# Side transfers issued in pieces between weight loads, and a norm's cross-channel sum four steps later, in a one-core hybrid decoder layer

## The chip, the core and the metric

One NeuronCore of a Trainium2 chip runs the whole layer. The metric is the device time of one execution in microseconds. Besides the repeated runs there is one execution taken with the hardware profiler; all rows of a view come from that one. In it the engines are TensorE (PE for the matmuls, PEld for its weight loads), VectorE (DVE), ScalarE (ACT), GpSimd (POOL) and SyncE (SP); a name with a q (SPq, ACTq) is an engine's sequencer, for example when it issues a DMA.

## The reference

For one sequence of 256 tokens of width 2048, in float32:

```
xn    = rms_norm(x, norm_mix_g)
proj  = xn @ w_in                     # u_s5, u_lru, q, k, v and three gates
gates = sigmoid(gate_logits + b_gate)
y_s5  = S5 branch: 64 groups, diagonal complex scan over time, gelu, GLU
y_lru = RG-LRU branch: causal conv, gated linear scan
y_att = stick-breaking attention, 8 heads of 128
merged = g_s5*(y_s5 @ w_br_s5) + g_lru*(y_lru @ w_br_lru) + g_attn*(y_att @ w_br_attn)
h  = x + merged @ w_out
h  = h + relu(rms_norm(h, norm_mlp_g) @ w_up)**2 @ w_down
out = rms_norm(h, final_norm_g)
```

## The kernel before

**The weight stream.** All weights are cut into 520 units of 256 x 512 values (512 KB), in one list that is also the order of use. A unit goes through four places. `load_next` (L130) issues its DMA on SP into one of three `raw` buffers. `split_next` makes two halves of it: ACT casts it to fp32r as `hi` (L146), DVE subtracts to get the rest, `lo` (L147); `hi` and `lo` have three buffers each. Then PE multiplies hi x hi, lo x hi and hi x lo: 12 matmuls of 512 columns for one unit (`chunk_tok`, L241 to L243; `pair_tok`, L276 to L278), or 24 of 256 (`chunk`, L225 to L227). A `raw` buffer is free once `lo` is made, and SP waits for that before the next load; `hi` and `lo` are free once PE is through with the unit. Units are numbered from 0 here: "unit 40" is the first of `w_br_lru`, "unit 232" the first of `w_out`, "unit 264" the first of `w_up`.

**Side work.** Everything else is written as generators. `later(gens, rate)` puts one on a list, and `pump()`, which is called after each unit, advances every listed generator by `rate` steps (a step ends at a `yield`). Each step is anchored behind the instructions of the unit just recorded. From this recorded program the framework's scheduler makes one fixed list for each engine at build time; SP's list is therefore one first-in, first-out queue in which weight loads and side transfers stand between each other, and an entry that waits holds all behind it.

**The places that the change touches.**

- `s5_scan`: for the first of eight blocks `s5_split(0)` makes `ux`, and `s5_stack(t)` for t = 0 to 3 copies parts of it into `stk` with three DMAs each (L627). PE's `ps_v` matmuls (L651) read `stk`, ACT copies their result to `s_v` (L653). For the later blocks the stacking is already spread over the steps of the scan.
- `gates`: for each of 12 chunks one row of `b_gate`, repeated over 128 partitions, is loaded to `gb` (L739, one buffer); DVE reads it when the chunk's matmuls are done (L744), and ACT takes the sigmoid (L745).
- the residual: `x_tok` (`xres` in the views), 2 MB, is loaded by one DMA on ACT's queue (L918) when the S5 pools are closed; DVE adds it to the result of `w_out` (L957). `gfb`, the last norm's gain repeated over 128 partitions (1 MB), is loaded by another one on ACT's queue (L989) and is first read near the end.
- `norm2`: the squares of the residual are summed by DVE over the channel tiles (L947, and two halvings at L972 in `hT`); then PE sums over partitions against a column of ones (`ps_n`, L977), and `rsqrt_mean` makes the scale `rs2`, which is not read before the first result of `w_down`.

Of the kernel before, what the change touches and what calls it, by code (L numbers as in the profile page):

```python
# [14 lines left out]
P = 128  # L15
# [3 lines left out]
CH = 512  # L19
# [27 lines left out]
def hybrid_block(ctx: ExitStack, tc: tile.TileContext, io, out):  # L47
    nc = tc.nc
# [115 lines left out]
    def later(gens, rate):  # L164
        side.append([deque(gens), rate, 0.0])
        return side[-1]
# [215 lines left out]
    def v2(t):  # L382
        return t.rearrange("p (a l) -> p a l", a=2)
# [10 lines left out]
    def repeat(a, n):  # L394
        r, w = a.shape
        return bass.AP(a.tensor, a.offset, [[w, r], [0, n], [1, w]])
# [219 lines left out]
    def s5_split(ct):  # L616
        bx = [ux[:, 2 + i, :].rearrange("p (r g s) -> p r g s", r=2, g=2) for i in range(2)]
        nc.scalar.copy(ux[:, 0, :], us5[:, ct, :])
        nc.vector.tensor_tensor(ux[:, 1, :], us5[:, ct, :], ux[:, 0, :].bitcast(F32), ALU.subtract)
        for g in range(2):  # L620
            m = mask[:, g:g + 1]
            nc.scalar.activation(bx[0][:, :, g, :], bco[:, ct], AF.Copy, scale=m)
            nc.vector.scalar_tensor_tensor(bx[1][:, :, g, :], bco[:, ct], m, bx[0][:, :, g, :].bitcast(F32), ALU.mult, ALU.subtract)
# [7 lines left out]
    def s5_scan():  # L631
        v = ypool.tile([P, 2, NT, L], F32, tag="yhi", name="s5_v")
        t12 = ypool.tile([P, 2, NT, L], F32, tag="ylo", name="s5_t")
        vr, vi, t1, t2 = v[:, 0], v[:, 1], t12[:, 0], t12[:, 1]
        tabs, more = s5_tables(0)
        yield from more
        s5_split(0)
        yield
        yield
        for t in range(NT):  # L640
            s5_stack(t)
        for _ in range(4):
            yield
        tt = nc.vector.tensor_tensor
        for b in range(WT):
            c, s = tabs
            t3 = pp.tile([P, NT, L], F32, tag="t3", name=f"t3_{b}")
            for t in range(NT):
                ps = pss.tile([P, CH], F32, tag="ps", name=f"ps_v{b}")
                for i in range(2):  # L650
                    nc.tensor.matmul(ps[:, i * L:(i + 1) * L], stk[:, t, 1, i * P:(i + 1) * P], stk[:, t, 0, :], start=i == 0, stop=True,  # L651
                                     skip_group_check=True)
                nc.scalar.copy(v[:, :, t, :], v2(ps))  # L653
                if t % 2:
                    yield
            more = iter(())
            if b + 1 < WT:
                s5_split(b + 1)
                tabs, more = s5_tables(b + 1)
                yield  # L660
            tt(t1, vr, c, ALU.mult)
            yield
            tt(t2, vi, s, ALU.mult)
            yield
            tt(t1, t1, t2, ALU.add)
            yield
            tt(t3, vi, c, ALU.mult)
            yield
            tt(vr, vr, s, ALU.mult)
            yield  # L670
            tt(t3, t3, vr, ALU.subtract)
            next(more, None)
            yield
            for x_ in (t1, t3):
                for t in range(NT):
                    j = b * NT + t
                    tt_scan(x_[:, t, :], rad[:, j:j + 1].broadcast_to([P, L]), x_[:, t, :])
                    if b + 1 < WT and x_ is t1:
                        s5_stack(t)
                    yield  # L680
            next(more, None)
            tt(t2, t1, c, ALU.mult)
            yield
            tt(vr, t3, s, ALU.mult)
            next(more, None)
            yield
            tt(t2, t2, vr, ALU.subtract)
            yield
            tt(vi, t3, c, ALU.mult)
            yield  # L690
            tt(t1, t1, s, ALU.mult)
            yield
            tt(t1, t1, vi, ALU.add)
            yield
            yield
            ps = pss.tile([P, CH], F32, tag="ps", name=f"ps_y{b}")
            for k, w_ in enumerate((t2, t1)):
                for t in range(NT):
                    nc.tensor.matmul(ps[t * 32:t * 32 + 32, 0:L], ce[:, k, b * NT + t, :, :], w_[:, t, :], start=k == 0, stop=k == 1,
                                     skip_group_check=True, tile_position=(0, t * 32))  # L700
            nc.vector.scalar_tensor_tensor(us5[:, b, :], us5[:, b, :], dsk[:, b:b + 1], ps[:, 0:L], ALU.mult, ALU.add)
            if b % 2:
                gq.append(later([gelu(b)], 1.0))
# [32 lines left out]
    def gates(idx, c, alloc):  # L736
        gb = tmp.tile([P, CH], F32, tag="gbias", name=f"gb{idx}_{c}", bufs=1)
        o = idx * D + c * CH
        nc.sync.dma_start(gb, repeat(io["b_gate_row"][:, o:o + CH], P))  # L739
        banks = chunk_tok("w_in", GATE0 + 4 * idx + c, D, xs)  # L740
        gts = []
        for j in range(2):
            g = alloc(c, j).rearrange("p a l -> p (a l)")
            nc.vector.scalar_tensor_tensor(g, banks[j], rstd_tok[:, j:j + 1], gb, ALU.mult, ALU.add)  # L744
            nc.scalar.activation(g, g, AF.Sigmoid)  # L745
            gts.append(g)
        return gts
# [118 lines left out]
    for q in range(4):  # L866
        s = slice(2 * q, 2 * q + 2)
# [4 lines left out]
    for c in range(2):  # L872
        banks = chunk("w_glu", c, W, lambda kt: (yg_hi[:, kt, :], yg_lo[:, kt, :]))
        for j in range(2):
# [4 lines left out]
            s = slice(c * 4 + 2 * j, c * 4 + 2 * j + 2)  # L879
# [22 lines left out]
    for a in S5_TAIL:  # L902
        c = int(a[1])
# [11 lines left out]
    mlp = ctx.enter_context(tc.tile_pool(name="mlp", bufs=1))  # L915
    gp = small("norm_mlp_g")
    x_tok = mlp.tile([P, 2, D], F32, name="xres")
    nc.scalar.dma_start(x_tok, io["x_res"])  # L918
    mf.append(chained(mq, split_tok(3, mlp.tile([P, 4, L], F32, tag="reluT", name="mT3", bufs=2))))
    hT = act.tile([P, KT, L], F32, tag="m16", name="hT")  # L920
    hhi = act.tile([P, KT, L], F32R, tag="xhi", name="hhi")
# [46 lines left out]
    def norm2():  # L968
        while rq[0]:
            yield  # L970
        for n in (2, 1):
            nc.vector.tensor_tensor(hT[:, 0:n, :], hT[:, 0:n, :], hT[:, n:2 * n, :], ALU.add)  # L972
        yield
        a = hT[:, 0, :]
        ps = pss.tile([P, CH], F32, tag="ps", name="ps_n2")
        for t in range(2):
            nc.tensor.matmul(ps[:, t:t + 1], a[:, t * P:(t + 1) * P], ones[:, 0:1], start=t == 0, stop=t == 1, skip_group_check=True)  # L977
        rsqrt_mean(rs2, ps[:, 0:2], 2)
        nc.vector.tensor_tensor(rs2, rs2, rs2, ALU.mult)
        yield  # L980

    tasks = [later([norm2()], 1.0)]


    gfb = mlp.tile([P, D], F32, name="gfb")
    ho = mlp.tile([P, 2, D], F32, name="ho")
    ssq = mlp.tile([P, 2, 6], F32, name="ssq")
    rf = mlp.tile([P, 2], F32, name="rf")
    nc.scalar.dma_start(gfb, repeat(io["final_norm_g"], P))  # L989

    def down_evac(t, s, bank):
        nc.vector.scalar_tensor_tensor(h_tok[:, t, s], bank, rs2[:, t:t + 1], h_tok[:, t, s], ALU.mult, ALU.add)
# [50 lines left out]
    for q in range(NQ):  # L1043
        hd, hf = {}, {}

        def up_done(cu, banks):
            c = cu % (FQ // CH)
            if c % 2 == 0:
                hd[c // 2] = (ypool.tile([P, WT, L], F32R, tag="yhi", name=f"hd_hi{q}_{c}"),
                              ypool.tile([P, WT, L], F32R, tag="ylo", name=f"hd_lo{q}_{c}"))  # L1050
            h_, l_ = hd[c // 2]
            r = mlp.tile([P, 2, CH], F32, tag="relu", name=f"relu{q}_{c}", bufs=2)
            for t in range(2):
                nc.scalar.activation(r[:, t, :], banks[t], AF.Relu)
            k = slice((c % 2) * 4, (c % 2) * 4 + 4)
            hf[c] = chained(hq, hidden(r, h_[:, k, :], l_[:, k, :], f"{q}_{c}"))

        if q == 0:
            pair_tok("w_up", 0, D, hs, up_done)
        for c in range(0 if q else 2, FQ // CH):  # L1060
            up_done(c, chunk_tok("w_up", q * (FQ // CH) + c, D, hs))

        def hs_(kt):
            need(hq, hf[kt // 4])
            h_, l_ = hd[kt // 8]
            return h_[:, kt % 8, :], l_[:, kt % 8, :]

        for task in tasks:
            finish(task)

        def down_done(c, banks):
            s = slice(c * CH, (c + 1) * CH)
            for t in range(2):
                down_evac(t, s, banks[t])
            if q == NQ - 1:
                for t in range(2):
                    square(t, s, c)
                    if c > 0:
                        total(t, c)
                    nc.gpsimd.tensor_tensor(ho[:, t, s], h_tok[:, t, s], gfb[:, s], ALU.mult)  # L1080

        pair_tok("w_down", 0, FQ, hs_, down_done)
        for c in range(2, 4):
            if q == NQ - 1 and c == 3:
                chunk_tok("w_down", c, FQ, hs_, HOLD, finish_tokens)
            else:
                down_done(c, chunk_tok("w_down", c, FQ, hs_))
# [67 lines left out]
```

## Time and profile before

| what | value |
|---|---|
| runs shown | 1517.03, 1522.82, 1524.22 us; median 1522.82 |
| profiled execution | 1518.29 us, of which the span from the first to the last instruction is 1516.4 us |
| PE / PEld busy | 1489.1 us (98%) / 1260.0 us (83%) |
| DVE / ACT / POOL busy | 1176.4 us (78%) / 783.9 us (52%) / 35.1 us (2%) |
| mean granted TensorE clock | 0.995 |
| DMA | 292.41 MB, mean 193 GB/s |

The profiled execution's own time is 1.9 us longer than its span, and 4.5 us under the median of the runs. A busy PE is not a PE at its peak: its matmuls overlap, so that one is recorded with about 390 ns while the next one starts 227 ns after it. A wait of PE is seen in the step from one matmul's start to the next one's.

### The profile page before, as it was taken

The numbers are of one execution on the slowest core, as the hardware profiler recorded it, in microseconds if no ns is written. First come the engines' busy times: TensorE is split into PE (matmuls) and PEld (weight loads), VectorE is DVE, ScalarE is ACT, GpSimd is POOL, SyncE is SP. The second block draws the span as 40 slices with busy tenths as digits, with TensorE's granted clock in tenths as the row PEclk, the third lists the DMA queues.
The fourth block names the chain that finished last, engine by engine and source line by source line (L and its number), as shares of the span: only waits on it lengthen the run. The fifth ranks groups of instructions, "written<-read, shape, count | busy, mean of one in ns | idle before, by whom it ended". The sixth has DMA issues, their size and how long they took to land.

```text
span 1516.4 us, 19895 instructions
## 1 busy us (share of the span) xinstructions
PE 1489.1 (98%) x7518; PEld 1260.0 (83%) x7518; DVE 1176.4 (78%) x1468; ACT 783.9 (52%) x920; POOL 35.1 (2%) x60
## 2 busy tenths in 40 slices
PE   9998999999999999999999999999999999999997
PEld 9996888989887878988787888888888888888886
DVE  6767988897988989689699797568855787558965
ACT  6767556565765564544355444344433444344443
POOL 1400000000000000000000000000000000000011
PEclk9999999999999999999999999999999999999999
DMA  9445766655555756565756556666666666666664
GB/s 291 152 151 180 214 205 201 187 182 170 176 174 179 211 185 210 185 204 187 268 179 189 185 181 207 194 191 198 193 195 192 192 190 198 191 194 192 193 196 152
DMA packets 88914, 292.41 MB, mean 193 GB/s; under 512 B 12786, under 2 KB 17010, under 8 KB 88562
## 3 DMA queue, kind: packets, MB, share of 16 engines
q1 hardware_dynamic: 88386, 287.93, 61.0%
q10 hardware_dynamic: 432, 3.21, 0.6%
q8 instruction: 59, 0.97, 0.3%
q14 instruction: 37, 0.30, 0.1%
HBM read 282.71 MB, written 2.10 MB: 188 GB/s over the span
## 4 chain that ended last, share of the span: by engine, by line
PE 81%; DVE 11%; issue 4%; ACT 2%; DMA 2%; SPq 0%; DVEq 0%; ACTq 0%
PE mt_w_up L242 6%; PE mt_w_up L243 6%; PE mt_w_up L241 6%; PE mt_w_in L242 5%; PE mt_w_in L243 5%; PE mt_w_in L241 5%; DVE lo L147 4%; PE mt_w_down L242 4%; PE mt_w_down L241 4%; PE mt_w_down L243 4%; PE mp_w_down L277 4%; PE mp_w_down L278 4%; PE mp_w_down L276 4%; PE mm_w_in L227 4%; PE mm_w_in L225 4%
## 5 line engine op out<-in xcount | busy, mean ns | idle before, releaser
L146 ACT CAST hi<-raw 128x1024 fp32r<-128x1024 f32 (+1 forms) x521 | 546.4, 1051 | 629.6 <-PE mt_w_up L243 131.6
L147 DVE TENSOR_TENSOR lo<-raw,hi 128x1024 fp32r<-128x1024 f32 (+1 forms) x521 | 638.2, 1226 | 289.4 <-ACT hi L146 285.6
L242 PE MATMUL mt_w_in<-lo,xhi 128*128 128x512 f32 x448 | 176.0, 393 | 3.5 <-DVE lo L147 3.4
L241 PE MATMUL mt_w_in<-hi,xhi 128*128 128x512 f32 x448 | 175.0, 395 | 0.2 <-ACT hi L146 0.2
L243 PE MATMUL mt_w_in<-hi,xlo 128*128 128x512 f32 x448 | 175.1, 391 | 0.0
L241 PE MATMUL mt_w_up<-hi,hhi 128*128 128x512 f32 x448 | 174.3, 389 | 0.0
L242 PE MATMUL mt_w_up<-lo,hhi 128*128 128x512 f32 x448 | 174.3, 389 | 0.0
L243 PE MATMUL mt_w_up<-hi,hlo 128*128 128x512 f32 x448 | 174.3, 389 | 0.0
L227 PE MATMUL mm_w_in<-xhi,lo 128*128 128x256 f32 x512 | 145.4, 286 | 4.7 <-DVE lo L147 4.7
L225 PE MATMUL mm_w_in<-xhi,hi 128*128 128x256 f32 x512 | 146.5, 286 | 0.4 <-ACT hi L146 0.4
L226 PE MATMUL mm_w_in<-xlo,hi 128*128 128x256 f32 x512 | 145.7, 285 | 0.0
L729 DVE STREAM_TRANSPOSE reluT<-relu 32x256 f32<-32x256 f32 x256 | 111.5, 435 | 4.2
L242 PEld LDWEIGHTS mt_w_in<-lo,xhi 128*128 128x128 f32 x448 | 84.6, 189 | 23.2 <-DVE lo L147 6.7
L227 PEld LDWEIGHTS mm_w_in<-xhi,lo 128*128 128x128 f32 x512 | 98.7, 194 | 5.7 <-DVE lo L147 5.7
L242 PE MATMUL mt_w_down<-lo,hd_hi 128*128 128x512 f32 (+1 forms) x272 | 102.5, 377 | 0.0
L241 PE MATMUL mt_w_down<-hi,hd_hi 128*128 128x512 f32 (+1 forms) x272 | 102.4, 377 | 0.0
L243 PE MATMUL mt_w_down<-hi,hd_lo 128*128 128x512 f32 (+1 forms) x272 | 102.4, 376 | 0.0
L277 PE MATMUL mp_w_down<-lo,hd_hi 128*128 128x512 f32 x256 | 99.8, 390 | 0.1
L225 PEld LDWEIGHTS mm_w_in<-xhi,hi 128*128 128x128 f32 x512 | 99.1, 194 | 0.9 <-ACT hi L146 0.7
L276 PE MATMUL mp_w_down<-hi,hd_hi 128*128 128x512 f32 x256 | 99.6, 389 | 0.0
L278 PE MATMUL mp_w_down<-hi,hd_lo 128*128 128x512 f32 x256 | 99.6, 389 | 0.0
L226 PEld LDWEIGHTS mm_w_in<-xlo,hi 128*128 128x128 f32 x512 | 99.2, 194 | 0.1
(299 smaller groups left out, 2356.1 us busy)
## 6 DMA issues: line engine op xcount, KB each, us to landing
raw<-in_w_in SPq DMA_DIRECT2D x175, 512.0 KB, 4.2
raw<-in_w_up SPq DMA_DIRECT2D x128, 512.0 KB, 4.3
raw<-in_w_down SPq DMA_DIRECT2D x128, 512.0 KB, 4.2
raw<-in_w_out SPq DMA_DIRECT2D x32, 512.0 KB, 4.2
raw<-in_w_br_lru SPq DMA_DIRECT2D x16, 512.0 KB, 4.2
raw<-in_w_br_attn SPq DMA_DIRECT2D x16, 512.0 KB, 3.9
raw<-in_w_br_s SPq DMA_DIRECT2D x16, 512.0 KB, 4.2
stk<-ux SPq DMA_DIRECT2D x96, 64.0 KB, 4.0
```

The costliest lines, as they stand in the source:

```text
L146: anchor["act"] = nc.scalar.copy(h[:, k, :], r[:, k, :]).ins
L147: anchor["dve"] = nc.vector.tensor_tensor(l_[:, k, :], r[:, k, :], h[:, k, :].bitcast(F32), ALU.subtract).ins
L225: nc.tensor.matmul(o, wh[:, kk, s], xh, start=first and ct % 2 == 0, stop=False, skip_group_check=True)
L226: nc.tensor.matmul(o, wh[:, kk, s], xl, start=False, stop=False, skip_group_check=True)
L227: mm = nc.tensor.matmul(o, wl[:, kk, s], xh, start=False, stop=last and ct % 2 == 1, skip_group_check=True)
L241: nc.tensor.matmul(banks[j], xh[:, s], wh[:, a:b], start=kt == 0, stop=False)
L242: nc.tensor.matmul(banks[j], xh[:, s], wl[:, a:b], start=False, stop=False)
L243: return nc.tensor.matmul(banks[j], xl[:, s], wh[:, a:b], start=False, stop=kt == ng * UK - 1)
L276: nc.tensor.matmul(o, xh[:, s], wh[:, kk, :], start=kt == 0, stop=False)
L277: nc.tensor.matmul(o, xh[:, s], wl[:, kk, :], start=False, stop=False)
L278: mm = nc.tensor.matmul(o, xl[:, s], wh[:, kk, :], start=False, stop=kt == ng * UK - 1)
L729: nc.vector.transpose(d_[32 * a:32 * a + 32, :, :, 32 * b:32 * b + 32], s_[32 * b:32 * b + 32, :, :, 32 * a:32 * a + 32])
```

## The change

Five edits, and nothing that is computed changes. The first block's stacking is issued with one step between the four groups of three DMAs. The gate's bias row is loaded by a side step three units after the chunk's start and no longer ahead of it. `x_tok` is loaded in four pieces of 512 KB on SP's queue, four steps apart, and no longer by one DMA on ACT's. `gfb` is loaded from SP and written at the second quarter of the MLP. And `norm2` has four steps, no longer one, between the sum over channel tiles and PE's sum over partitions.

```diff
@@ s5_scan
         for t in range(NT):
             s5_stack(t)
-        for _ in range(4):
             yield
@@ gates
         gb = tmp.tile([P, CH], F32, tag="gbias", name=f"gb{idx}_{c}", bufs=1)
         o = idx * D + c * CH
-        nc.sync.dma_start(gb, repeat(io["b_gate_row"][:, o:o + CH], P))
+
+        def bias():
+            for _ in range(3):
+                yield
+            nc.sync.dma_start(gb, repeat(io["b_gate_row"][:, o:o + CH], P))
+            yield
+
+        later([bias()], 1.0)
         banks = chunk_tok("w_in", GATE0 + 4 * idx + c, D, xs)
@@ residual
     x_tok = mlp.tile([P, 2, D], F32, name="xres")
-    nc.scalar.dma_start(x_tok, io["x_res"])
+
+    def x_load():
+        for c in range(4):
+            s = slice(c * CH, (c + 1) * CH)
+            nc.sync.dma_start(x_tok[:, :, s], io["x_res"][:, :, s])
+            for _ in range(4):
+                yield
+
+    later([x_load()], 1.0)
@@ norm2
             nc.vector.tensor_tensor(hT[:, 0:n, :], hT[:, 0:n, :], hT[:, n:2 * n, :], ALU.add)
-        yield
+        for _ in range(4):
+            yield
         a = hT[:, 0, :]
@@ the last norm's gain
-    nc.scalar.dma_start(gfb, repeat(io["final_norm_g"], P))
...
+        if q == 1:
+            nc.sync.dma_start(gfb, repeat(io["final_norm_g"], P))
         pair_tok("w_down", 0, FQ, hs_, down_done)
```

What the built programs make of it is seen at three places. First SP's queue at the first block's stacking, before; `raw_1508` is the load of unit 39 and `raw_1538` that of unit 40, and a first DMA of the stacking stands ahead of these rows:

```order
L130 DMA raw_1508<-in_w_in 128x1024
L627 DMA stk<-ux 32x512
L627 DMA stk<-ux 32x2x256 x2
L627 DMA stk<-ux 32x512
L627 DMA stk<-ux 32x2x256 x2
L627 DMA stk<-ux 32x512
L627 DMA stk<-ux 32x2x256 x2
L627 DMA stk<-ux 32x512
L627 DMA stk<-ux 32x2x256
L130 DMA raw_1538<-in_w_br_lru 128x1024
L130 DMA raw_1556<-in_w_br_lru 128x1024
L130 DMA raw_1574<-in_w_br_lru 128x1024
```

Eleven stacking DMAs stand between the loads of units 39 and 40. The same place of SP's queue in the changed program, where unit 40 is `raw_1529`:

```order
L130 DMA raw_1508<-in_w_in 128x1024
L627 DMA stk<-ux 32x512
L627 DMA stk<-ux 32x2x256
L130 DMA raw_1529<-in_w_br_lru 128x1024
L627 DMA stk<-ux 32x2x256
L627 DMA stk<-ux 32x512
L627 DMA stk<-ux 32x2x256
L130 DMA raw_1550<-in_w_br_lru 128x1024
L627 DMA stk<-ux 32x2x256
L627 DMA stk<-ux 32x512
L627 DMA stk<-ux 32x2x256
L130 DMA raw_1571<-in_w_br_lru 128x1024
```

Two stacking DMAs now stand ahead of unit 40, three more ahead of each of units 41, 42 and 43. At the same place ACT's list, before, from the cast of unit 38 (`hi_1510`) to that of unit 42 (`hi_1611`):

```order
L146 CAST hi_1510<-raw_1484 128x1024
L146 CAST hi_1540<-raw_1508 128x1024
L745 ACT_TABLE_LOAD
L745 ACTIVATE gate_0_0_1601<-gate_0_0_1601 128x512
L745 ACTIVATE gate_0_1_1604<-gate_0_1_1604 128x512
L146 CAST hi_1558<-raw_1538 128x1024
L146 CAST hi_1576<-raw_1556 128x1024
L653 COPY s_v<-ps_v_1593 128x2x256
L653 COPY s_v<-ps_v_1597 128x2x256
L146 CAST hi_1611<-raw_1574 128x1024
```

And in the changed program (its line numbers are up to 16 higher; L652 is L653 of before, L751 is L745):

```order
L146 CAST hi_1510<-raw_1483 128x1024
L146 CAST hi_1531<-raw_1508 128x1024
L146 CAST hi_1552<-raw_1529 128x1024
L146 CAST hi_1573<-raw_1550 128x1024
L652 COPY s_v<-ps_v_1593 128x2x256
L652 COPY s_v<-ps_v_1597 128x2x256
L751 ACT_TABLE_LOAD
L751 ACTIVATE gate_0_0_1601<-gate_0_0_1601 128x512
L751 ACTIVATE gate_0_1_1604<-gate_0_1_1604 128x512
L146 CAST hi_1611<-raw_1571 128x1024
```

The casts of units 40 and 41 have moved ahead of the gate's sigmoid. On DVE the `lo` of unit 40 has likewise moved ahead of the gate's two L744. Behind unit 42 two more copies of `ps_v` (the third and fourth pair) now stand ahead of the cast of unit 43, which stood ahead of them.

The second place is the start of `w_out`. Before, the two large transfers stand in ACT's list; `hi_6651` is the cast of unit 235:

```order
L146 CAST hi_6651<-raw_6631 128x1024
L918 DMA xres<-in_x_res 128x4096
L146 CAST hi_6673<-raw_6649 128x1024
L146 CAST hi_6693<-raw_6671 128x1024
L146 CAST hi_6715<-raw_6691 128x1024
L989 DMA gfb<-in_final_norm_g 128x1x2048
L146 CAST hi_6735<-raw_6713 128x1024
```

In the changed program they stand in SP's queue; `raw_6649` is the load of unit 236:

```order
L130 DMA raw_6649<-in_w_out 128x1024
L928 DMA xres<-in_x_res 128x2x512
L130 DMA raw_6671<-in_w_out 128x1024
L130 DMA raw_6691<-in_w_out 128x1024
L130 DMA raw_6713<-in_w_out 128x1024
L928 DMA xres<-in_x_res 128x2x512
L130 DMA raw_6734<-in_w_out 128x1024
L928 DMA xres<-in_x_res 128x2x512
L130 DMA raw_6756<-in_w_out 128x1024
L130 DMA raw_6776<-in_w_out 128x1024
L928 DMA xres<-in_x_res 128x2x512
L130 DMA raw_6794<-in_w_out 128x1024
```

The pieces follow units 236, 239, 240 and 242. `gfb`, although it is written at the second quarter of the MLP, is the next row, between units 243 and 244: nothing but free memory holds it, and the scheduler has put it here.

The third place is PE's list at the second norm. Before, in the first 12 matmuls of unit 273 (`hi_7476`):

```order
L277 MATMUL mp_w_up_1_264_7320<-lo_7454,hhi 128x512
L278 MATMUL mp_w_up_1_264_7320<-hi_7453,hlo 128x512
L276 MATMUL mp_w_up_0_264_7319<-hi_7476,hhi 128x512
L277 MATMUL mp_w_up_0_264_7319<-lo_7477,hhi 128x512
L977 MATMUL ps_n_7513<-ones,hT 128x1 x2
L278 MATMUL mp_w_up_0_264_7319<-hi_7476,hlo 128x512
```

In the changed program, between unit 275 (`hi_7517`) and unit 276 (`hi_7535`):

```order
L277 MATMUL mp_w_up_1_264_7322<-lo_7518,hhi 128x512
L278 MATMUL mp_w_up_1_264_7322<-hi_7517,hlo 128x512
L992 MATMUL ps_n_7569<-ones,hT 128x1 x2
L276 MATMUL mp_w_up_0_264_7319<-hi_7535,hhi 128x512
L277 MATMUL mp_w_up_0_264_7319<-lo_7536,hhi 128x512
```

The sum over partitions comes 34 matmuls later; DVE's L972 stay where they were. Of the twelve bias rows, eight stand at the same place of SP's queue as before; the second and fourth of the RG-LRU gates stand three loads and one load later, the second and fourth of the attention gates four loads and one load later.

## The prediction

> **What bounds the kernel now.** I read the page first, then PE's own waits, and then, at each wait that the change can reach, the timeline of the engines that end it.
>
> ```profile
> span 1516.4 us, 19895 instructions
> PE 1489.1 (98%) x7518; PEld 1260.0 (83%) x7518; DVE 1176.4 (78%) x1468; ACT 783.9 (52%) x920; POOL 35.1 (2%) x60
> ```
>
> PE is the bound nearly throughout: a gain can only come out of the time in which it waits or runs slowly. From the view of waits for PE (in total us, how often, longest), three rows of twelve:
>
> ```profile
> PE ps_n L977 <- DVE hT L972: 2.3, 1, 2.3
> PE mt_w_br_attn L241 <- ACT hi L146: 2.2, 1, 2.2
> PE mt_w_br_lru L241 <- ACT hi L146: 2.0, 1, 2.0
> ```
>
> The change reaches the `ps_n` row, the `mt_w_br_lru` row (first unit after the stacking) and two smaller waits at the start of `w_out` (below); the `mt_w_br_attn` row lies in an ACT order that the change leaves alone. A wait can cost more than itself, which the granted clock shows (each row: stretch, its length, busy time and instruction starts of PE, PEld, DVE, ACT, POOL, then the clock's share, DMA share and GB/s):
>
> ```profile
> 143.80:147.10 3.30, 3.17 (x7) 2.07 (x8) 2.58 (x3) 3.00 (x5) 0.00 (x0) 0.50 0.66 226
> 486.00:489.40 3.40, 3.10 (x12) 2.25 (x13) 3.33 (x3) 1.93 (x3) 0.00 (x0) 1.00 0.28 83
> 834.70:838.10 3.40, 3.40 (x17) 2.89 (x18) 1.51 (x5) 0.94 (x3) 0.00 (x0) 1.00 0.76 211
> 155.70:170.70 15.00, 15.00 (x68) 12.43 (x67) 14.98 (x16) 5.28 (x5) 0.00 (x0) 1.00 0.72 210
> ```
>
> Behind the `mt_w_br_lru` wait PE ran 3.3 us at half clock; behind the other two, though as long, at full clock. The last row has PE undisturbed: 68 matmuls in 15.00 us, about 0.22 to 0.23 us from start to start, so 2.7 us for a unit of twelve.
>
> **First block's stacking.** The stacking's DMA row (KB each, median us to landing), then SP, ACT and PE around unit 40:
>
> ```profile
> stk<-ux SPq DMA_DIRECT2D x96, 64.0 KB, 4.0
> 131.71 7.04 SPq L627 DMA_DIRECT2D stk<-ux  x11
> 138.79 1.56 SPq L130 DMA_DIRECT2D raw<-in_w_br_lru  x3
> 135.13 1.28 ACT L745 ACT_TABLE_LOAD   x1
> 141.59 1.31 ACT L745 ACTIVATE gate<-gate 128x512 f32<-128x512 f32 x2 [5.18 <-DVE gate L744]
> 142.81 2.13 ACT L146 CAST hi<-raw 128x1024 fp32r<-128x1024 f32 x2
> 141.29 0.64 PE L651 MATMUL ps_v<-stk 96*128 96x256 f32 x4
> 143.89 1.22 PE L241 MATMUL mt_w_br_lru<-hi,ylru_hi 128*128 128x512 f32 x2 [1.97 <-ACT hi L146]
> ```
>
> Eleven stacking issues of 7.04 / 11 = 0.64 us keep SP until 138.75, so three weight loads leave together at 138.79. Behind that the cast of unit 40 also stands after a sigmoid that waits for the end of the gate's chunk (5.18 us). PE waits 1.97 us, then starts 7 matmuls in a 3.30 us stretch where 7 x 0.23 = 1.6 is usual: another 1.7 lost, 3.7 in all. After the change two issues stand ahead of unit 40, which leaves at 131.71 + 2 x 0.64 = 133.0; in the trace it left at 138.79 and was cast at 142.81, at most 4.0 us later, so its cast can now be made at 137 and, being ahead of the sigmoid, is. Units 41 and 42 leave after three more issues each, at about 135.4 and 137.7, and land by 139.4 and 141.7, ahead of PE. What is late next: the second group of `stk`, which PE's `ps_v` wants at 141.29, is out by 135.3 and lands 4.0 us later, 139.3; it hides by 2 us. The 3.7 us wait is gone, but not all is kept, because DVE is full a little later:
>
> ```profile
> 148.92 1.05 ACT L146 CAST hi<-raw 128x1024 fp32r<-128x1024 f32 x1 [2.07 <-PE ps_v L651]
> 153.00 1.23 DVE L147 TENSOR_TENSOR lo<-raw,hi 128x1024 fp32r<-128x1024 f32 x1 [0.77 <-ACT hi L146]
> 155.72 1.23 DVE L147 TENSOR_TENSOR lo<-raw,hi 128x1024 fp32r<-128x1024 f32 x1 [0.35 <-ACT hi L146]
> 168.88 1.20 DVE L147 TENSOR_TENSOR lo<-raw,hi 128x1024 fp32r<-128x1024 f32 x1
> 170.98 0.39 PE L242 MATMUL mt_w_in<-lo,xhi 128*128 128x512 f32 x1
> ```
>
> From 155.7 to 170.7 (the window above) DVE is busy 14.98 of 15.00 us, with the scan's products beside the `lo`. The `lo` of unit 49 is ready at 170.08 and used at 170.98: PE may come 0.90 us earlier and no more, unless DVE does too. DVE can close its idle 0.77 + 0.35 = 1.1 us ahead of the full stretch; it can't start earlier, since the cast of unit 43, at 148.92 now, will stand behind copies of the `ps_v` that PE makes inside unit 42: 141.9 + 2 x 2.7 + 0.7 = 148.0, so about 149 again. Kept: 0.9 + 1.1 = 2.0 us. Bounds: 0.9 (DVE gains nothing) and 3.7 (all kept); I take 2.0, built from this stretch's own rows.
>
> **Residual and last gain.** Two DMA rows (KB each, us to landing), then ACT, SP and PE:
>
> ```profile
> xres<-in_x_res ACTq DMA_DIRECT2D x1, 2048.0 KB, 8.6
> raw<-in_w_out SPq DMA_DIRECT2D x32, 512.0 KB, 4.2
> 719.80 0.33 ACTq L918 DMA_DIRECT2D xres<-in_x_res  x1
> 721.46 1.06 ACT L146 CAST hi<-raw 128x1024 fp32r<-128x1024 f32 x1 [1.66 <-PE mp_w_out L278]
> 729.08 1.05 ACT L146 CAST hi<-raw 128x1024 fp32r<-128x1024 f32 x1 [6.57 <-DMA raw<-in_w_out]
> 720.88 0.33 SPq L130 DMA_DIRECT2D raw<-in_w_out  x1
> 729.19 0.39 PE L278 MATMUL mp_w_out<-hi,mg_ylo 128*128 128x512 f32 x1
> 730.18 0.50 PE L276 MATMUL mp_w_out<-hi,mg_yhi 128*128 128x512 f32 x1 [0.60 <-ACT hi L146]
> 731.44 0.50 PE L277 MATMUL mp_w_out<-lo,mg_yhi 128*128 128x512 f32 x1 [0.76 <-DVE lo L147]
> 734.08 0.39 PE L276 MATMUL mp_w_out<-hi,mg_yhi 128*128 128x512 f32 x1
> 734.51 0.50 PE L277 MATMUL mp_w_out<-lo,mg_yhi 128*128 128x512 f32 x1
> ```
>
> The 2 MB leave at 719.80; unit 237's load, issued 1.1 us later, is cast only at 729.08, 8.2 us after its issue against a usual 4.2: 4.0 us late. PE's steps 729.19, 730.18, 731.44 are 0.99 and 1.26 long where 0.23 is usual, so 1.8 us are lost, and at 734.08 to 734.51 another 0.2. A piece is a quarter of that size; a quarter of 4.0 us is 1.0, and ACT has 1.66 us in hand here (it waited for PE to free a buffer). So no piece should reach PE. The first piece waits, as before, for the S5 pools to be free near 719.8, with unit 237's load behind it; that load wasn't to leave until 720.88, so the wait costs nothing. `gfb`, 1 MB, is worth half of 4.0, 2.0 us, spread over loads whose casts run a buffer ahead; it stands seven loads behind the first piece and hides if the 1.66 us and the `hi` in hand (another unit, 2.7 us) last. Worth 2.0 us; bounds 0 (pieces delay as much in sum as the whole) and 2.0. I take 2.0, since the nearest row, 1.66 us of ACT waiting for PE, is larger than the delay of a piece.
>
> [...]
>
> **Second norm.**
>
> ```profile
> 831.93 0.39 PE L277 MATMUL mp_w_up<-lo,hhi 128*128 128x512 f32 x1
> 834.66 0.58 PE L977 MATMUL ps_n<-ones,hT 128*128 128x1 f32 x4 [2.35 <-DVE hT L972]
> 831.10 1.23 DVE L947 TENSOR_TENSOR hT<-hT 128x1024 f32<-128x1024 f32 x1
> 834.10 0.42 DVE L972 TENSOR_TENSOR hT<-hT 128x256 f32<-128x256 f32 x1
> ```
>
> The step from 831.93 to 834.66 is 2.73 us long, 2.5 too much. PE stands at `ps_n` with unit 273 behind it, though the last L972 ends only at 834.52. 34 matmuls later is 34 x 0.23 = 7.8 us later, near 840: DVE is done 5 us before. Behind `ps_n` nothing is late: `rs2` isn't read before `w_down`. Late next would be the `lo` of unit 274, which DVE makes just ahead of the last L972, so by about 834.2; PE wants it at 831.93 + 12 x 0.23 = 834.7. Worth 2.5 us; bounds 2.0 (0.5 us is that margin) and 2.5; I take 2.5.
>
> **Gate rows.** SP's wait for the row's buffer, and one place of it:
>
> ```profile
> SPq L739 <- DVE gate L744: 16.1, 9, 3.2
> 180.87 0.53 SPq L739 DMA_DIRECT2D gb<-in_b_gate_row  x1
> 182.00 2.54 SPq L130 DMA_DIRECT2D raw<-in_w_in  x2
> ```
>
> SP waits 16.1 us for these, but at 180.87 the row leaves, and the next weight load waits until 182.00 for its own buffer: SP stood idle anyway. Only four of twelve rows move. I take 0, within 0.5 either way (one issue of 0.53 us).
>
> **Sum.** 2.0 + 2.0 + 0 + 2.5 = 6.5 us, by bounds 2.4 to 8.7. The profiled execution, 1518.3 us, would become 1511.8. It is 4.5 us below the median 1522.8; the four executions shown average 1520.6, and from there I predict 1514. What a measurement of this kernel can tell from no change is about 0.5%, 7.6 us, and the sum lies just inside.
>
> **Rivals.**
> - *More than forecast: half clock spared elsewhere, and nothing handed back.* A half-clock stretch costs 1.7 us. In this trace it followed one of three waits of 2.0 to 2.35 us, so in other executions it may follow the `ps_n` wait or the one at `w_out`; with either or both, and 1.7 us not handed back at 170 us, the gain is 8 to 11 us: 1512.6 down to 1509.6. Against it: DVE's 14.98 of 15.00. [...]
> - *Part of it.* Pieces and `gfb` still hold weight loads up, or the stacking keeps its lower bound 0.9: 2.5 to 5 us gained, 1516 to 1518.
> - *Slower.* Five transfers now stand in SP's own queue, ahead of weight loads. If each costs PE as much as the one of 2 MB did (2.0 us), 10 us are lost where 2.0 were, and with 4.5 gained elsewhere the time is 1520.6 + 3.5 = 1524. It decides at a delay for each piece above ACT's 1.66 us plus the unit in hand, about 4 us; a whole 2 MB made 4.0. To be slower by 7.6 the delays would have to be near 7 us each.
> - *The gate rows do matter.* If SP's 16.1 us were on PE's path, up to that much more is gained: 1498. Against it: the load behind waits for its buffer.
>
> **Chances.** Forecast (5.5 to 8.0 us) 0.50; more 0.16; part 0.28; slower 0.04; gate rows 0.02. Executions differ by several us, so I count a third of the forecast's chance, most of "more" and the gate rows as faster by over 0.5%: 0.36. Slower by over 0.5%: 0.03; the rest, 0.61, within it. The range takes the fastest execution shown less the larger gain (1517 - 11 = 1506) to the slowest less the lower bound (1524.2 - 2.4 = 1521.8).
>
> **What would show it.** Right: no wait of PE at unit 40 and no half clock near 144 us; a new small wait for `lo` between units 46 and 49; the first casts of `w_out` waiting for PE, not for DMA; no `ps_n` row among PE's waits. Wrong: PE waiting for `raw` behind the pieces or `gfb`, for `stk` at the first `ps_v`, or no wait at 160 to 170 us, by which the hand-back would have been an error.

## The result, and the profile after

The changed kernel ran in 1511.40 us (median of 4, 1510.79 to 1512.10) against 1521.38 us for before beside it (1517.03 to 1524.22): a ratio of 0.9938, 95% interval 0.9918 to 0.9957. A second comparison, with more executions, gave 1510.67 against 1518.70 us, 0.9940 (0.9925 to 0.9954). (The ratio is the comparison's own estimate; it is not the quotient of the two medians, which would be 0.9947.) So it is about 0.6% or 8 to 10 us faster: below the forecast of 1514.0, inside the range, and, by its middle though not by its whole interval, on the side of "faster by over 0.5%", which had 0.36 and not the largest chance. The two profiles differ by less, 1518.3 and 1512.1 us, 6.2 us where the sum said 6.5. What the 2 to 4 us between these two readings are is the question of the experiments.

The page and PE's longest waits, of after (in total us, how often, longest):

```profile
span 1510.3 us, 19900 instructions
PE 1488.4 (99%) x7518; PEld 1260.5 (83%) x7518; DVE 1175.2 (78%) x1468; ACT 782.3 (52%) x920; POOL 35.3 (2%) x60
```
```profile
PE mm_w_in L227 <- DVE lo L147: 4.5, 5, 1.9
PE mt_w_in L242 <- DVE lo L147: 3.7, 5, 1.9
PE mt_w_br_attn L241 <- ACT hi L146: 2.2, 1, 2.2
```

`ps_n` and `mt_w_br_lru` no longer stand among the waits. The four stretches that the prediction showed, after (same columns):

```profile
143.80:147.10 3.30, 3.30 (x17) 2.76 (x16) 0.31 (x1) 3.29 (x5) 0.00 (x0) 1.00 0.81 264
155.70:170.70 15.00, 14.51 (x63) 11.34 (x63) 15.00 (x16) 6.03 (x6) 0.00 (x0) 1.00 0.72 221
486.00:489.40 3.40, 3.40 (x11) 2.69 (x10) 3.40 (x4) 0.00 (x0) 0.00 (x0) 0.64 0.71 204
834.70:838.10 3.40, 3.40 (x18) 2.87 (x17) 1.22 (x1) 0.83 (x2) 0.00 (x0) 1.00 0.73 263
```

At 144 us there is full clock; at 156 to 171 us PE now has gaps and 63 matmuls where it had 68, with DVE at 15.00 of 15.00 us; and at 486 us, which the change doesn't touch, there is half clock where before had none. The three places in the timeline of after (SP, ACT and PE around unit 40; PE's new wait and its start of unit 50; then `w_out`; then `ps_n`):

```profile
133.09 0.58 SPq L130 DMA_DIRECT2D raw<-in_w_br_lru  x1
138.11 1.05 ACT L146 CAST hi<-raw 128x1024 fp32r<-128x1024 f32 x1 [3.18 <-DMA raw<-in_w_br_lru]
141.36 0.64 PE L650 MATMUL ps_v<-stk 96*128 96x256 f32 x4
141.84 0.40 PE L241 MATMUL mt_w_br_lru<-hi,ylru_hi 128*128 128x512 f32 x1
160.19 0.50 PE L242 MATMUL mt_w_in<-lo,xhi 128*128 128x512 f32 x1 [0.42 <-DVE lo L147]
171.14 0.39 PE L241 MATMUL mt_w_in<-hi,xhi 128*128 128x512 f32 x1
...
718.68 0.57 SPq L928 DMA_DIRECT2D xres<-in_x_res  x1
725.25 1.05 ACT L146 CAST hi<-raw 128x1024 fp32r<-128x1024 f32 x1 [4.02 <-DMA raw<-in_w_out]
728.13 0.39 PE L276 MATMUL mp_w_out<-hi,mg_yhi 128*128 128x512 f32 x1
...
836.27 0.50 PE L992 MATMUL ps_n<-ones,hT 128*128 128x1 f32 x4
```

And unit 50 in before:

```profile
173.47 0.39 PE L241 MATMUL mt_w_in<-hi,xhi 128*128 128x512 f32 x1
```

The load of unit 40 leaves at 133.09 (forecast 133.0), is cast at 138.11 (forecast 137), and PE goes on at 141.84. PE starts unit 50 at 171.14 where before started it at 173.47, though both stood at the same place ahead of unit 40 (`ps_v` at 141.36 and 141.29): 2.4 us kept, 2.0 forecast. The cast of unit 237 (at 725.25) still waits for its load (4.02 us), not for PE as forecast; but it ends 1.8 us before PE wants it, and PE's steps from one start to the next are even. `ps_n` runs without a wait.

For the experiments I add up PE's *lost time*: for each matmul, what its start is later than the usual step (0.227 us for 512 columns) after the one ahead of it, waits and half clock alike, over a stretch of PE's own work, so that kernels can be compared stretch by stretch.

### The profile page after: what moved, and what is told of

Its sections match the earlier page's. It is cut to its first block, busy times and chain, and to the rows that moved or that the text cites. A ratio compares the mean times of both kernels' runs of the same rounds, so it can differ in the third digit from the quotient of the medians.

```text
span 1510.3 us, 19900 instructions
## 1 busy us (share of the span) xinstructions
PE 1488.4 (99%) x7518; PEld 1260.5 (83%) x7518; DVE 1175.2 (78%) x1468; ACT 782.3 (52%) x920; POOL 35.3 (2%) x60
## 4 chain that ended last, share of the span: by engine, by line
PE 83%; DVE 9%; issue 3%; ACT 2%; DMA 2%; SPq 0%; DVEq 0%; ACTq 0%
PE mt_w_up L242 6%; PE mt_w_up L241 6%; PE mt_w_up L243 6%; PE mt_w_in L242 5%; PE mt_w_in L243 5%; PE mt_w_in L241 5%; PE mt_w_down L242 4%; PE mt_w_down L241 4%; PE mt_w_down L243 4%; PE mp_w_down L277 4%; PE mp_w_down L278 4%; PE mp_w_down L276 4%; PE mm_w_in L227 4%; PE mm_w_in L225 4%; PE mm_w_in L226 4%; DVE lo L147 3%
## 5 line engine op out<-in xcount | busy, mean ns | idle before, releaser
L241 PEld LDWEIGHTS mt_w_in<-hi,xhi 128*128 128x128 f32 x448 | 84.5, 189 | 17.8 <-ACT hi L146 0.7
```

What stands on the lines that cost most here:

```text
L241: nc.tensor.matmul(banks[j], xh[:, s], wh[:, a:b], start=kt == 0, stop=False)
```

## The experiments

**What makes executions differ: before, again.**

> The kernel before, unchanged, to see what makes its executions differ (1517.0 to 1524.2) and why the medians moved by 10 us where the two profiles moved by 6.2. Theory (half clock): in both profiles every half-clock stretch starts a whole number of 3.413 us steps after the one before it (37.55, 13.65 and 354.98 us are 11, 4 and 104 steps), and stands behind a step in which PE stood still for about 2.0 us or more (0.58 and above; 0.53 was not enough). Then a wait of 2.0 to 2.35 us is followed by half clock only when it falls into one step, and the executions differ in how many of the five such waits (near 90, 127, 141, 483, 832 us) are: times go with the mean granted clock, about 1.7 us for each 0.001 (3.413/2/1516 = 0.0011), and this profile shows half clock behind another set of the five. Rival (transfers): times differ by 2 us and more at the same granted clock, and the profile shows the difference as waits for DMA.

Measured: 1520.11 us (1517.31 to 1524.23), ratio 1.0002. Over the 75 executions of before in three comparisons, the 12 with a mean granted clock up to 0.992 took 1522.7 us on average (1521.6 to 1524.2), the 28 with 0.997 or more 1517.9 us (1515.6 to 1519.9); time and clock correlate at -0.90, 0.86 us for each 0.001, half of the 1.7 that was expected. The half clock fell on another set of waits, with the one at unit 40 in both. In every profile the stretches at half clock start whole multiples of 3.413 us apart (37.55 and 13.65 us, 11 and 4 of them, in the first one of before), and I call these the steps of the clock. This profile (first four rows), and the first one of before at `ps_n` (last two), cut at these steps:

```profile
483.36:486.77 3.41, 1.26 (x6) 0.58 (x4) 0.53 (x1) 3.40 (x4) 0.00 (x0) 1.00 0.21 80
486.77:490.18 3.41, 3.27 (x8) 2.40 (x8) 3.41 (x4) 1.33 (x2) 0.00 (x0) 0.50 0.49 147
...
834.93:838.34 3.41, 1.15 (x7) 1.10 (x8) 3.33 (x5) 2.59 (x3) 0.00 (x0) 1.00 0.53 159
838.34:841.76 3.42, 3.42 (x9) 2.69 (x9) 0.48 (x3) 0.10 (x1) 0.00 (x0) 0.50 0.80 265
```
```profile
829.83:833.25 3.42, 2.49 (x11) 1.71 (x10) 3.38 (x5) 2.63 (x3) 0.00 (x0) 1.00 0.67 205
833.25:836.66 3.41, 2.00 (x11) 1.76 (x12) 2.96 (x7) 1.97 (x3) 0.00 (x0) 1.00 0.60 189
```

The same `ps_n` wait lay in one step here (PE busy 1.15 of 3.41 us) and half clock followed; in the first profile a step's edge at 833.25 cut it in two (2.49 and 2.00 busy), and none followed. The rival, transfers, falls as the main cause.

**The parts alone**, each on before. Stacking: the loop of four steps ahead of `yield` goes, so that each `s5_stack(t)` has its own. Residual: `x_load`, and `gfb` at `q == 1`. Norm: `for _ in range(4): yield` ahead of `ps_n`.

> The kernel before with the stacking edit alone. Theory (hand-back): the wait and the half clock near 141 us are gone (3.7 us), new waits for lo of 1.2 to 1.7 us in sum stand at 146 to 170 us, PE is 2.0 to 2.3 us earlier at unit 50 (171.1 instead of 173.5 us), and nothing else changes: profile 1516 us. Rival (all kept): no new waits, 3.7 us. In the timed runs 1 to 3 us less than before, by how often the wait was followed by half clock.

> The kernel before with the residual's x in four pieces and the last gain later, and nothing else. Theory: PE's steps at 729 to 735 us are even again, 2.0 to 2.3 us less, no cast waits for raw at 721 to 730 us: profile 1516 us, no half clock concerned, so the timed runs too are 2.0 to 2.3 us under before. Rival (the delays are only spread): under 1 us.

> The kernel before with the sum of the second norm four steps later, and nothing else. Theory: no wait at ps_n, 2.5 us less in the profile at 832 us (1515.8 us), and in the timed runs 2.5 to 4 us less, since the wait of 2.35 us was followed by half clock in some executions of before. Rival (the wait goes to the lo behind it): 2.0 us or less.

Measured: 1517.85, 1517.77 and 1516.96 us against 1518.98: ratios 0.9990 (0.9978 to 1.0001), 0.9989 (0.9979 to 0.9999), 0.9986 (0.9977 to 0.9996). Each profile shows its place as forecast: in the first no wait ahead of unit 40 and 1.5 us of new lost time behind it; in the second 0.6 us lost in the first half of `w_out`, where before lost 2.6; in the third none at `ps_n`. But the second and the third gained less in the timed runs (1.2 and 2.0 us) than the 2.0 to 2.3 and 2.5 to 4 expected, and the profiles of the first and third came at 1518.7 and 1518.8 us, not at 1516, with four stretches of half clock each where before's first had three. In the medians the three sum to 4.3 us only.

**The whole again, and without one edit each.**

> The changed kernel again, to have its gain beside that of the parts on many executions. The parts alone gave medians 1.1 (stacking), 1.2 (residual) and 2.0 us (second norm) under the 1519.0 of before, 4.3 in sum; by means 1.8, 1.7 and 2.3, 5.8 in sum. Theory (the parts add up): 5 to 6.5 us under before, 0.33 to 0.43%. Rival (the first comparison, 10 us, holds because the parts help one another): 8 to 10 us. By the half-clock theory its times lie closer together than those of before, since two of the five waits of over 2 us are gone: spread 3 to 5 us instead of 8.

> The changed kernel with the stacking put back as before, so without the stacking edit alone. The whole change was 8.0 us faster than before in medians (0.9940 of it), the parts alone 4.3 in sum, and the profiles say why one edit may look smaller alone. Lost time of PE between 110 and 165 us of its work was 5.5 to 7.0 us in the four profiles without the stacking edit and 2.2 to 3.2 us in those with it. Theory (half clock counted): this kernel is 3 to 4 us slower than the changed one, 0.9964 of before. Rival (the prediction's 2.0 us): 0.9953. Rival (as alone, 1.1 us): 0.9947.

> The changed kernel without the edit of the second norm. At 820 to 840 us PE lost 2.6 us where its wait of 2.35 us was split by the grid of 3.413 us steps, and 4.1 us in the profiles in which half clock followed (3 of 4). Theory: 2.5 to 4.1 us slower than the changed kernel, by how often half clock follows, 0.9965 of before; the profile shows either 2.6 or 4.1 to 4.2 us lost there. Rival (the prediction's 2.5 at all times): 0.9956.

> The changed kernel without the edit of the gate rows. Profiles of kernels with and without it agree within 0.4 us on what PE loses between 165 and 650 us of its work. Theory (prediction: 0, within 0.5): the time of the changed kernel within 0.5 us, 0.994 of before. Rival (the gate rows are what the parts alone lack, 2 to 3 us): 0.9957.

Measured, each as a ratio to before beside it: whole 0.9940 (0.9925 to 0.9954); without stacking 0.9969 (0.9955 to 0.9983); without norm 0.9974 (0.9962 to 0.9986); without gate rows 0.9943 (0.9929 to 0.9957). In medians the gain is 8.0 us with all edits, 4.3 without stacking, 4.1 without norm, 7.8 without gate rows: they are worth 3.7, 3.9 and 0.2 us in this company, and 1.1 and 2.0 alone for the first two. That points to the rival of the first expectation, parts that help one another. It isn't shown beyond doubt: each part alone is known to about 1.6 us either way and the whole to 2.2, together (root of the summed squares) some 3.5 us, and the gap between 8.0 and 4.3 is 3.7, or 3.1 by means (8.9 and 5.8). One thing that makes the worth of the stacking edit differ between executions shows in PE's waits of the kernel without it:

```profile
PE mt_w_br_lru L241 <- ACT hi L146: 2.8, 1, 2.8
```

It is 2.8 us here where the prediction's row has 2.0. In the two profiles without the stacking edit in which no half clock fell on the 16 us ahead of unit 40 (this one and before's second), PE lost 2.8 us in them against 3.7 to 4.7 in the three others, and then 2.9 and 3.3 us at unit 40 against 2.1 to 2.3. In these two the cast of unit 40 waits 0.69 and 1.05 us for its load, which leaves behind the stacking, so what is won ahead of it is lost there; in the three others it stands right behind the sigmoid, which waits for PE's own chunk. The residual and the norm lie behind unit 40, so this doesn't explain what they gain in company.

**What makes the clock fall.** 36 waits, put into after between units of `w_up` and `w_down`; the next unit's matmuls are queued behind them:

```
nc.tensor.matmul(pp_[:, 0:1], ones, ones[:, 0:1], start=True, stop=True, ...)
nc.scalar.copy(x_tok[:, 1, 0:1], pp_[:, 0:1])
nc.scalar.activation(x_tok[:, 1, 0:n], x_tok[:, 0, 0:n], AF.Copy, scale=x_tok[:, 1, 0:1])
nc.tensor.matmul(pp_[:, 1:2], x_tok[:, 1, n - P:n], ones[:, 0:1], start=True, stop=True, ...)
```

> The changed kernel with 36 waits of PE put between units of w_up and w_down, where it has none: a matmul of one column, an ACT copy of its result, an ACT product of 640, 1024, 1280, 1536, 1792 or 2048 columns in turn, and a matmul of one column that waits for it, so 1.1 to 3 us each. It measures what makes the clock fall. Theory (fixed steps): each half-clock stretch starts on one grid of 3.413 us, and stands behind a step of that grid in which PE stood still for 1.95 us or more; so none follows a wait under 1.9 us, about half of those of 2.2 us and 2 of 3 of those of 2.8 us are followed, and which ones can be told from the grid. Rival (length alone): all waits over 2 us. [...]

It took 1665.0 us in its one execution. All half-clock stretches of this profile start on one grid of 3.413 us. Pairs of steps, a wait in the first, the second with the clock that followed:

```profile
1291.65:1295.06 3.41, 1.47 (x9) 1.23 (x8) 2.37 (x5) 1.93 (x3) 0.00 (x0) 1.00 0.48 156
1295.06:1298.48 3.42, 3.42 (x10) 2.65 (x9) 0.79 (x2) 0.00 (x0) 0.00 (x0) 0.50 0.47 153
...
1230.21:1233.62 3.41, 1.67 (x9) 1.32 (x7) 3.24 (x4) 1.79 (x3) 0.00 (x0) 1.00 0.66 234
1233.62:1237.04 3.42, 2.48 (x12) 2.12 (x13) 0.48 (x1) 0.89 (x1) 0.00 (x0) 1.00 0.63 193
...
970.80:974.21 3.41, 2.05 (x11) 1.65 (x9) 1.59 (x2) 1.71 (x4) 0.00 (x0) 1.00 0.58 193
974.21:977.62 3.41, 2.51 (x12) 2.12 (x13) 0.86 (x1) 0.84 (x1) 0.00 (x0) 1.00 0.65 217
```

Counted over all 14 profiles of this study, 5957 full-clock steps between 20 and 1490 us: the 49 in which PE was busy for less than 1.64 us of the 3.41 were all followed by half clock, of the 5889 with more than 1.87 us none, of the 19 between 5. (The two borders are drawn from this count, not forecast; 1.64 us of work is 1.77 of standing still, under the 1.95 that was expected.) So the rival falls: in these profiles a wait's length alone does not decide. Four of the waits of 2.3 to 2.7 us put in were not followed: a step's edge cut each, and no part was over 1.77 us. The wait at 483 us of after, in its first profile and in the second:

```profile
481.64:485.05 3.41, 1.04 (x5) 0.31 (x3) 0.99 (x1) 3.40 (x5) 0.00 (x0) 1.00 0.08 26
485.05:488.47 3.42, 3.42 (x8) 2.74 (x9) 3.42 (x4) 0.88 (x1) 0.00 (x0) 0.50 0.51 153
```
```profile
478.34:481.75 3.41, 2.05 (x10) 1.35 (x8) 0.00 (x0) 3.39 (x5) 0.00 (x0) 1.00 0.44 166
481.75:485.17 3.42, 2.40 (x9) 1.71 (x10) 2.65 (x3) 2.64 (x3) 0.00 (x0) 1.00 0.19 26
```

**The waits filled.** Ahead of the matmul that waits at 90, 127 and 483 us of after:

```
for _ in range(5):
    f = tc.keep_in_program_order(nc.tensor.matmul(o[:, 0:P], ones, ones, start=True, stop=True, ...))
```

> The changed kernel with five matmuls of 128 columns (1.15 us, their result is not used) put into PE's row at each of the three places where it waits over 2 us, near 90, 127 and 483 us; one or two matmuls of 0.11 and 0.23 us that used to run ahead of the wait come behind it. Theory (fixed steps of 3.413 us, 1.95 us of standing still): PE now stands still for 1.0 to 1.4 us only, no half clock is left in the profile, the mean granted clock is at the top of its range in all executions, and the time falls by 0.5 to 2 us (each wait costs up to 1.7 us more in about half the executions; up to 0.45 us is given back by the order) and its spread to under 2 us. Rival (half clock only goes along with waits and costs nothing by itself): the time is the same or 0.3 to 0.5 us longer.

One of the places (ten records for the five matmuls), with the clock's steps at the wait:

```profile
479.61 1.28 PE L220 MATMUL fill<-ones 128*128 128x128 f32 x10
481.91 0.77 PE L255 MATMUL mt_w_br_attn<-hi,ya_hi 128*128 128x512 f32 x2 [1.03 <-ACT hi L146]
480.16:483.57 3.41, 2.19 (x12) 1.43 (x11) 1.68 (x2) 3.41 (x4) 0.00 (x0) 1.00 0.00 0
483.57:486.98 3.41, 3.41 (x17) 2.78 (x16) 3.41 (x4) 0.45 (x2) 0.00 (x0) 1.00 0.65 178
```

Without the filling PE would have been busy for 1.46 us of the first step (2.19 less the 0.73 us of the filling that lie in it), less than any step that full clock followed. (At 90 and 127 us it would have been busy for over 2.1 us of each step even without, so there this one profile shows nothing.) The first half holds: no half clock in the profile, and a mean clock of 0.998 or more in all six executions, where the ten of after had 0.995 to 0.998. The second does not: 1511.62 us, 0.9946 (0.9930 to 0.9962), nothing gained on 1510.67, as the rival had it. The two profiles of after say the same: the one with half clock at all three places has a span of 1510.3 us, that with none 1508.9, 1.4 us for all three. Up to 171 us PE runs into later waits for DVE's `lo` (DVE is busy 15.00 of 15.00 us from 155.7 us on, above), which take up what it loses. In these runs half clock was dearer where nothing ended later anyway: behind `ps_n` it cost 1.6 us by PE's lost time.

**Splitting or the queue.** In after, `nc.sync.dma_start(x_tok, io["x_res"])` as one transfer at the first piece's place.

> The changed kernel with the residual's x as one transfer of 2 MB, but on SP's queue at the place of the first piece. It tells splitting from the change of queue. Theory (splitting counts): the load behind it lands 4 us late as in before, and 1.5 to 2.3 us come back at 728 to 735 us. Rival (the queue counts): nothing comes back, and PE's steps there are even.

```profile
726.40 1.04 ACT L146 CAST hi<-raw 128x1024 fp32r<-128x1024 f32 x1 [6.94 <-DMA raw<-in_w_out]
727.49 0.73 PE L276 MATMUL mp_w_out<-hi,mg_yhi 128*128 128x512 f32 x2 [0.97 <-ACT hi L146]
```

The 6.57 us for which ACT waited in before are back as 6.94, with 2.6 us lost by PE from 726 to 732 us; the time is 1513.51 us, 0.9960 (0.9945 to 0.9975), 2.8 us over the change, though the two intervals overlap a little. From issue to landing unit 237's load took 8.2 us here, 8.1 in before and 5.4 with the pieces, so splitting is what counts here. (`gfb` too left early here, at 722.56 us; but in before it left only at 730.38, behind that landing, and the load was as late.)

**Two more orders.** The experiments pointed to the wait at 483 us: ACT makes a sine, a sigmoid and a cosine of the S5 tables, with a table load of 1.28 us ahead of each, while unit 151 stands behind. In `s5_scan`, and in `lru_half`:

```
             tt(vr, t3, s, ALU.mult)
-            next(more, None)
+            if b != 5:
+                next(more, None)
...
             tt(vi, t3, c, ALU.mult)
+            next(more, None)
...
+            if c:
+                yield
             nc.scalar.copy(ylru_hi[:, s, :], xc)
```

(The call behind `vi` does nothing in the other blocks, whose steps are used up.)

> The changed kernel with two more pieces of work moved, at the two waits of over 2 us that an order of ACT or DVE makes: the third step of the S5 tables of one block, two steps later, so that two casts and the gate's sigmoid come ahead of it and a table load less is made (wait of 2.31 us near 482 us), and the copy and rest of the last LRU half, one step later, so that the lo of unit 36 comes ahead of them (wait of 2.07 us near 127 us). Theory: the first wait goes (2.3 us, and 0.8 us of half clock in half of the executions), and of the second 1.3 us, of which DVE, full until 170 us, may hand back all: 2.5 to 4 us under the changed kernel, 1507.5 us, 0.992 of before. Rival (both are handed back, or the cast of unit 151 then waits for something else): the time of the changed kernel.

```profile
span 1504.0 us, 19901 instructions
```
```profile
477.50 1.06 ACT L146 CAST hi<-raw 128x1024 fp32r<-128x1024 f32 x1 [0.82 <-ACT gate L755]
478.46 1.05 ACT L611 ACTIVATE tc<-ts 128x1024 f32<-128x1024 f32 x1
479.53 1.28 ACT L612 ACT_TABLE_LOAD   x1
```

1506.06 us, 0.9910 (0.9895 to 0.9925): 4.6 us under the changed kernel's 1510.67, a little more than the 2.5 to 4 expected, and the fastest here. The cast of unit 151 now stands ahead of the tables, and no wait for `mt_w_br_attn` is left; lost time from 400 to 500 us of work falls from 7.1 to 3.0 us. The LRU half brought nothing: by 165 us of its work PE had lost 20.2 us, against 20.4 in the changed kernel's second profile: DVE handed it back.

## Why the prediction was right, and where its sizes were off

- **Stacking** (2.0; bounds 0.9 to 3.7). The mechanism held: the early load, the new small waits for `lo`, and the hand-back, 1.5 to 1.9 us of new lost time in all seven profiles that have the edit and no other one near it, against 0 in the five without (1.7 forecast). The profile pair gave 2.4. Over all profiles, lost time from 110 to 165 us of work was 5.9 us on average without the edit and 2.8 with it: 3.1, and 3.7 by the times. The step that was too small is "the 3.7 us wait": with its half clock it took 4.0 to 6.4 us of lost time in the five profiles that have it, the most (5.0 and 6.4) where PE came early and waited for the load behind the stacking.
- **Residual and last gain** (2.0). Right in size: 2.3 us on average in three profiles without the edit against those with it, and 4.0 in the one of before where half clock fell on this place too. Undone in part (one transfer), 2.8 us. "The first casts waiting for PE" was wrong. The piece made unit 237's load 1.2 us late (1.0 forecast), but its cast waited 4.02 us for it, so the 1.66 us of ACT that the prediction counted on were not in hand there; PE's own lead hid it, with 1.8 us left.
- **Second norm** (2.5). Right for the profile pair, too small on average. "At full clock" was true of that one execution: the `ps_n` wait was followed by half clock in three of the five profiles that have it. Those lose 6.2 us from 740 to 800 us of work, the two others 4.6, and kernels with the edit 2.1: 4.1 or 2.5 us, 3.4 on average, and 3.9 by the times.
- **Gate rows** (0, within 0.5): 0.2 us, in a comparison good to about 2 us. SP waited 13.5 us for the rows without this edit and 12.0 with it, and nothing of that reached PE.
- **The rivals.** "Slower" and the gate rows fall. "More than forecast", at 8 to 11 us, comes nearest to the measured 8 to 10 us, by the first half of its mechanism: half clock is spared at `ps_n` and at `w_out`. Its second half, nothing handed back, is wrong. I had the mechanism and gave it too little: I priced each term at one execution's clock, though that trace held equal waits with and without half clock. Priced at half the executions, 1.5 us of half clock behind `ps_n` alone would have added 0.8.
- The profile pair's 6.2 against 6.5 is less of a confirmation than it looks: that execution of before was spared half clock at `ps_n`, and after's had it at 483 us.

**Open.** Alone the parts gained 4.3 us in medians, together 8.0, a gap hardly clear of the noise, and no run here shows its cause. I can't say whether the grid of steps falls evenly on the executions of each kernel: the second norm alone, the same program up to 830 us, had no execution of 12 with a clock of 0.997 or more, and the residual alone one of 12, where 28 of 75 of before had.

## What to carry to other kernels

A wait of PE is priced with the chance of half clock behind it (at `ps_n` in three of five profiles here, 4.1 us lost and not 2.5), and one profile shows one draw of that: compare the granted clock of all executions before a term is taken from one. The stall at unit 40, whose end the load behind the stacking set, swallowed what was won ahead of it (2.9 and 3.3 us lost there in two profiles, 2.1 to 2.3 in the three others), so remove such stalls first. Half clock where PE waits for a full DVE a little later was nearly free here (1.4 us for three stretches); look at what ends next before spending work on it.

## What the runs showed of the hardware that I had not expected

- In the 14 profiles here the stretches at half clock start whole multiples of 3.413 us apart, and two executions of before have the steps at different places (an edge at 833.25 us in one, at 834.93 and 838.34 us in the other). Behind a step with under 1.64 us of PE busy the next ran at half clock in 49 of 49 cases, behind one with over 1.87 us in none of 5889. The wait of 2.35 us at `ps_n`, cut by a step's edge, cost nothing more. Behind a wait within one step, the matmuls in the step at half clock started 1.4 to 1.9 us later in sum than usual.
- With 1.28 us of matmuls whose result nobody uses put ahead of the wait near 483 us, PE was busy for 2.19 us of the step (1.46 without them, by my estimate) and full clock followed. With such matmuls at three waits all six executions had a mean clock of 0.998 or more, where the ten of after had 0.995 to 0.998.
